# Output block products of an encoder layer: an earlier copy of a norm vector, a load in its place, and a new order of reads, gates and offsets

## The chip, the cores and the metric

The kernel runs on one core of a Trainium2 chip. The metric is the device time of one execution in microseconds (us). Five engines work side by side, each in the order of its own instructions: TensorE (PE; its weight loads are PEld), VectorE (DVE), ScalarE (ACT), GpSimd (POOL) and SyncE (SP), which only issues DMAs here. They wait for each other by semaphores.

## What is computed

The reference is one layer of a bidirectional encoder: an input projection, gated linear attention and latent attention side by side, then one output projection and a layer norm with a scaled residual. For this change the end matters:

```
mixed = concatenate([o_a, o_b], axis=-1) @ w_out        # 2048 x 1024 @ 1024 x 1024
x = layer_norm(DEEPNORM_ALPHA * x + mixed, ln_g, ln_b)
```

## The kernel before

Each float32 operand is split in a high part (a rounding copy, `K.hi`, mostly on ScalarE, line 396) and a low part (the rest, `K.lo`, mostly on GpSimd, line 402), and a product is three matmuls (`mm3`, lines 450 to 452): high x high, high x low, low x high.

The output projection works on 16 chunks of 128 rows. Chunks 0 to 7 are whole products: 2 halves of 512 columns, 8 blocks of 128 rows of the weights, 48 matmuls each. Chunks 8 to 15 go in four pairs (class `Pair`), pair p being chunks 9 + 2p (row 0) and 8 + 2p (row 1). A pair is a 2x2 block product made with seven half-size products instead of eight (12 matmuls each): A11 and A12 are the two attention outputs of row 0, A21 and A22 those of row 1, and

- S1 = A21 + A22, S3 = A11 - A21, S2 = S1 - A11, S4 = A12 - S2 are adds on VectorE (`add`, line 2016). S2 and S4 overwrite A11, S3 overwrites A21.
- The products in their order are P1 (operand A11), P5 (S1), P6 (S2), P3 (S4), P7 (S3), P2 (A12), P4 (A22); in the last pair P2 stands before P7 and P4 comes in two halves. They write the PSUM banks `pw`: P1 bank 0, P5 bank 1, P6 bank 2, P3 bank 3, P7 bank 0, P2 bank 1, P4 bank 3.
- VectorE adds them to the residual (`read`, lines 2051 and 2053: R1, R5, R5b, R2, R6, R3, R7, R4, R4b; U2 and U3, line 2044, combine two products in a bank). A bank can be written again only after its reads: P4 after R6 (the read of P3), P5 of the next pair after R7 (the read of P2).

P5 to P7 use weight combinations prepared earlier and fetched by `fetch_t` (names "1h" to "3l"); P4 uses "4h" and "4l", which overwrite half of `W`. "3l" lies in two tiles, `wt3l` and `wt3m`.

`Pair.load` brings a row's two attention outputs (`of`, from `oa_s` and `ob_s`) and its gates (`gr`, from `gm_s` and `r_s`) with four DMAs from SP. For pairs 0 and 2 `of` is a tile of a pool; for pairs 1 and 3 it is the place of the layer norm's vectors, `lng` for row 0 and `lnb` for row 1, free once `ln_psum` (line 2203, ScalarE) has copied them into PSUM. The `gr` of a row is the same place in every pair. `Pair.gate` (line 2004, GpSimd) multiplies the second attention output by the two gates.

The end of a chunk is a mean and variance, `finish_a` (lines 2312 to 2315, and `rsqrt`, lines 2321 to 2326 on ScalarE) or `squares`, `scale` and `centre` for row 0 of a pair, then `finish_b` (line 2332, VectorE): times the inverse deviation plus the offset `ln_b`, and a DMA to the output for each half. Row 0 of the last pair ends instead with `finish_first` (lines 2094 and 2095): ScalarE multiplies, GpSimd adds the offset from `lnbc`, a copy in SBUF (`copy_lnb`, line 2088).

The order is written out by hand. `PLACE_PAIR` gives each step of a pair a place in us relative to the pair's start T; all steps from chunk 6 on are sorted by place and held in that order on all five engines. The steps before (chunks 4 and 5, `split`, `finish`) are in program order on ScalarE, GpSimd and SP only. The places set the order alone: an engine waits for whatever its next instruction needs.

Of the kernel before, what the change touches and what calls it, by code (L numbers as in the profile page):

```python
# [9 lines left out]
F32 = mybir.dt.float32  # L10
F32R = mybir.dt.float32r
# [16 lines left out]
QB = 512  # L28
NQB = S // QB
NKT = S // P  # L30
# [65 lines left out]
    rcp=13.55,  # L96
# [11 lines left out]
    hi=(10.43, 11.83, 12.21, 14.39, 15.18, 22.96, 28.7, 34.03),  # L108
    lo=(15.35, 16.07, 20.38, 20.41, 24.45, 25.82, 33.5, 36.25),
# [24 lines left out]
PAIR0, PAIR_US = 8, 19.05  # L134
PLACE_PAIR = dict(
    load=(-31.0, -31.5),
    load1=(-23.6, -35.9),
    res=(-10.0, -8.0),
    gate=((-19.94, -18.58), (-24.72, -21.3)),
    add=dict(S1=-10.55, S3=-9.85, S2=-8.0, S4=-4.37),  # L140
    hi=dict(A11=-17.26, S1=-9.75, S2=-7.3, A12=-5.39, S3=-4.77, S4=-3.53, A22=-2.66),
    lo=dict(A11=-13.14, S1=-8.45, S2=-6.6, S3=-3.67, A22=1.77, A12=3.13, S4=4.49),
    product=dict(P1=0.0, P5=2.72, P6=5.44, P3=8.16, P7=10.88, P2=13.6, P4=16.32),
    last=dict(P1=0.0, P5=2.72, P6=5.44, P3=8.16, P2=10.88, P7=13.6, P4=16.32),
    gate1=((-14.6, -13.3), (-19.95, -18.6)),
    gate0=((-6.0, -4.7), (-24.72, -21.3)),
    first=dict(hA11=-15.2, hS3=-8.0, hA12=-2.6, lS3=-6.5, lS4=-2.2),
    read=dict(c1=2.78, R1=5.9, R5=6.5, R5b=7.1, U2=9.9, R2=10.5, R6=11.87, c7=14.91, U3=15.63, R3=16.26, bn22=16.89,
              R7=17.52, sq=18.25, R4=20.34, R4b=20.97, bn21=21.6, rs=21.9, fa=(22.9, 22.23), fb=(23.9, 26.7)),
    read_last=dict(c1=2.78, lnb=9.0, R1=3.3, R5=6.3, R5b=6.9, U2=8.9, R2=9.5, R3=10.1, R4b=10.7, R6=11.5, bn12=12.1,  # L150
                   R7=14.1, bn11=14.7, R3p=16.9, R4p=17.5, bn22=18.1, fa=(15.3, 20.2), fb=(17.0, 20.3)),
)

# [30 lines left out]
    vh=(0.732, 1.218),  # L184
# [26 lines left out]
    vl=(0.859, 1.227),  # L211
# [174 lines left out]
class K:  # L386
# [1215 lines left out]
    def attention(self):  # L1602
# [4 lines left out]
        with ExitStack() as ctx:  # L1607
# [220 lines left out]
            def put(place, fn, *a):  # L1828
                todo.append((place, len(todo), fn, a))
# [139 lines left out]
class Pair:  # L1969
# [12 lines left out]
    def load(self, r):  # L1982

        kern, nc, c = self.k, self.nc, self.c[r]
        b, cs = c // 4, slice((c % 4) * P, (c % 4 + 1) * P)
        if self.p % 2:
            of = self.op.ln_sb[r].rearrange("p a (b d) -> p a b d", b=4)
        else:
            of = kern.xfp.tile([P, 2, 4, P], F32, tag="xf", name=f"of{c}")
        self.of[r] = of  # L1990
        gr = self.rows[r]["gr"] = self.op.gr[c % 2]
        nc.sync.dma_start(of[:, 0], kern.oa_s[c])
        nc.sync.dma_start(gr[:, 0], kern.gm_s[b][:, :, cs])
        nc.sync.dma_start(gr[:, 1], kern.r_s[b][:, :, cs].to_broadcast([P, 4, P]))
        nc.sync.dma_start(of[:, 1], kern.ob_s[b][:, :, cs])
# [94 lines left out]
    def finish_first(self):  # L2090
        o, c = self.rows[0], self.c[0]
        for n in range(2):
            rr = o["rr"][:, n]
            self.nc.scalar.activation(rr, rr, AF.Copy, scale=o["rs"])
            self.nc.gpsimd.tensor_tensor(rr, rr, self.lnb[:, n], ALU.add)
            self.nc.sync.dma_start(self.k.out[c * P:(c + 1) * P, n * 512:(n + 1) * 512], rr)

    def put(self, put, T, last):
        at = lambda place, fn, *a: put(T + place, fn, *a)
        P_, op = PLACE_PAIR, self.op  # L2100
        first = {} if self.p else P_["first"]
        if self.p:
            for r in (1, 0):
                at(P_["load1" if self.p == 1 else "load"][r], self.load, r)
        for r in range(2):
            at(P_["res"][r], self.load_res, r)
            for n in range(2):
                at(P_[f"gate{self.p}" if self.p < 2 else "gate"][r][n], self.gate, r, n)
        for n in self.OPERANDS:
            if n[0] == "S":  # L2110
                at(P_["add"][n], self.add, n)
# [31 lines left out]
        at(e["lnb"], self.copy_lnb)  # L2143
# [14 lines left out]
class OutProj:  # L2158
# [47 lines left out]
    def fetch_t(self, n):  # L2206


        j, p = int(n[0]), "hl".index(n[1])
        src, kern = self.k.wt_s[j][p], self.k  # L2210
        if j == 4:
            for k in range(4):
                self.nc.sync.dma_start(self.W[k][p][:, 512:].bitcast(F32), src[:, k])
            return
        if n == "3l":
            t = [kern.wof.tile([P, D], F32R, tag="raw", name="wt3l", bufs=1).rearrange("p (a d) -> p a d", a=2),
                 kern.keep.tile([P, 2, QB], F32R, tag="acc", name="wt3m")]
            for i in range(2):
                self.nc.sync.dma_start(t[i].bitcast(F32), src[:, 2 * i:2 * i + 2])
        else:  # L2220
            slot = dict(zip(("1h", "1l", "2h", "2l", "3h"), ("ckvT_h", "ckvT_l", "krs", "vh", "vl")))[n]
            t = kern.rp.tile([P, NKT, P], F32R, tag=f"res_{slot}", name=f"wt{n}").rearrange("p (k a) d -> p k (a d)", k=4)
            self.nc.sync.dma_start(t.bitcast(F32), src)
            t = [t[:, 0:2], t[:, 2:4]]
        self.T[j, p] = t
# [67 lines left out]
    def residual(self, o, n):  # L2293
        nc, c = self.nc, o["c"]
        if n == 0:
            o["rr"] = self.bp.tile([P, 2, 512], F32, tag="ph", name=f"rr{c}", bufs=3)
            o["bn"] = self.sm.tile([P, 2, 6], F32, tag="bn", name=f"bn{c}")
        rr = o["rr"][:, n]
        nc.vector.scalar_tensor_tensor(rr, o["xr"][:, n], ALPHA, o["ps"][n], ALU.mult, ALU.add)
        nc.vector.bn_stats(o["bn"][:, n], rr)  # L2300

    def finish(self, o):
        self.finish_a(o)
# [98 lines left out]
```

## Time and profile before

| | us |
|---|---|
| median of 3 runs (1286.0 to 1287.68) | 1286.68 |
| the profiled execution | 1286.29 |
| its span, first to last instruction | 1284.5 |
| chunk 4 to the end, from | 1149.17 |
| pair 0 begins on TensorE | 1194.14 |
| pairs 1, 2, 3 begin | 1217.01, 1236.26, 1255.30 |
| last matmul begins | 1274.62 |

The times of instructions are counted from the start of the span, so the profiled execution is 1.8 us longer than what its trace shows. A line of a timeline gives the start, the duration, the engine, the line of the kernel, the operation, the tiles (out<-in), the shapes and the count, and in brackets the idle time before it and what ended it. A line of the DMA queue (SPq) is the issue; the transfer lands later.

### The profile page before, as it was taken

The page shows a single profiled execution, that of the slowest core. Times are in us where ns is not written, and L with a number is a line of the kernel's source. Part 1 is how long each engine was busy: PE and PEld are TensorE (multiplying, and loading weights), DVE is VectorE, ACT ScalarE, POOL GpSimd, SP SyncE. Part 2 cuts the span into 40 slices and gives each one's busy share as a digit, 9 for nine tenths or more (in the row PEclk, how much of TensorE's full clock was granted, in tenths as well). Part 3 has the DMA queues.
Part 4 walks back from the last instruction along what each step waited for, and adds up shares of the span by engine and source line. Part 5 has one row for each costly group of instructions (what it writes and reads, how often), then busy time and mean ns, then how long its engine had stood idle before and what let it go on. Part 6 is the DMA issues. An engine that isn't in the chain of part 4 may idle for free.

```text
span 1284.5 us, 20176 instructions
## 1 busy us (share of the span) xinstructions
PE 1257.6 (98%) x6928; PEld 1110.4 (86%) x6928; DVE 941.5 (73%) x1706; ACT 874.0 (68%) x1549; POOL 846.9 (66%) x546
## 2 busy tenths in 40 slices
PE   7999999999999999999999999999999999999997
PEld 7999999999889999999788888888888888888785
DVE  6865775656675455555798888888888888658788
ACT  7765657666675656665688888888888888614454
POOL 0244555363667666672188888889999999955762
PEclk9999999999999999999999999999999999999998
DMA  9332525353675565565501111122123211469952
GB/s 298 97 93 63 173 74 170 89 155 101 197 243 166 183 220 182 180 207 163 164 1 41 42 42 41 42 58 59 57 58 92 68 55 34 170 188 309 356 183 80
DMA packets 122518, 166.81 MB, mean 130 GB/s; under 512 B 18502, under 2 KB 71118, under 8 KB 121776
## 3 DMA queue, kind: packets, MB, share of 16 engines
q1 hardware_dynamic: 114256, 163.39, 40.2%
q0 software_dynamic: 768, 2.10, 0.5%
q8 instruction: 55, 0.90, 0.4%
q10 hardware_dynamic: 7392, 0.03, 0.3%
q14 instruction: 47, 0.39, 0.2%
HBM read 106.72 MB, written 58.75 MB: 129 GB/s over the span
## 4 chain that ended last, share of the span: by engine, by line
PE 56%; POOL 4%; issue 3%; DMA 3%; DVE 3%; ACT 3%; SPq 0%; DVEq 0%; POOLq 0%; ACTq 0%
PE pS L1636 4%; PE o L452 4%; PE o L450 4%; PE o L451 4%; PE pS L1637 4%; PE pS L1638 4%; PE pS L1639 4%; PE pS L1640 4%; PE pz L451 2%; PE pz L452 2%; PE pz L450 2%; PE ipm L452 1%; PE ipm L450 1%; PE ipm L451 1%; PE po L451 1%
## 5 line engine op out<-in xcount | busy, mean ns | idle before, releaser
L402 POOL TENSOR_TENSOR pl<-s,ph 128x1024 fp32r<-128x1024 f32 x128 | 306.1, 2416 | 56.6 <-ACT ph L396 56.6
L1658 DVE TENSOR_TENSOR rm<-pS,rm 128x512 f32<-128x512 f32 x210 | 144.8, 689 | 26.5 <-ACT s L1645 20.9
L1682 DVE TENSOR_TENSOR s<-s,mb 128x1024 f32<-128x1024 f32 x128 | 151.2, 1213 | 9.4 <-PE mb L1676 9.3
L1645 ACT ACTIVATE s<-pS 128x1024 f32<-128x1024 f32 x128 | 131.4, 1027 | 37.7 <-PE pS L1640 33.5
L396 ACT ACTIVATE ph<-s 128x1024 fp32r<-128x1024 f32 x128 | 134.9, 1057 | 13.5 <-PE o L452 12.9
L1686 ACT ACTIVATE s<-s 128x1024 f32<-128x1024 f32 x128 | 131.5, 1051 | 13.4 <-DVE s L1682 13.3
L450 PE MATMUL ipa<-wah,xah 128*128 128x384 f32 (+1 forms) x384 | 130.2, 339 | 6.1 <-ACT wah L396 6.0
L1099 POOL TENSOR_TENSOR Us<-Us,cw 128x512 f32<-128x512 f32 x16 | 18.6, 1163 | 174.2 <-DVE Us L1097 158.7
L451 PE MATMUL ipa<-wal,xah 128*128 128x384 f32 (+1 forms) x384 | 125.1, 326 | 0.2 <-DVE wal L402 0.2
L452 PE MATMUL ipa<-wah,xal 128*128 128x384 f32 (+1 forms) x384 | 125.2, 326 | 0.0
L1636 PE MATMUL pS<-qh,ckvT_h 128*128 128x512 f32 x256 | 102.6, 401 | 0.8 <-DVE rm L1658 0.4
L450 PE MATMUL o<-ph,vh 128*128 128x512 f32 x256 | 101.1, 395 | 0.0
L1637 PE MATMUL pS<-ql,ckvT_h 128*128 128x512 f32 x256 | 99.9, 390 | 0.0
L1638 PE MATMUL pS<-qh,ckvT_l 128*128 128x512 f32 x256 | 99.9, 390 | 0.0
L1639 PE MATMUL pS<-rh,krs 128*128 128x512 f32 x256 | 99.8, 390 | 0.0
L1640 PE MATMUL pS<-rl,krs 128*128 128x512 f32 x256 | 99.8, 390 | 0.0
L452 PE MATMUL o<-ph,vl 128*128 128x512 f32 x256 | 99.8, 390 | 0.0
L451 PE MATMUL o<-pl,vh 128*128 128x512 f32 x256 | 99.7, 389 | 0.0
L1709 DVE TENSOR_TENSOR ap<-ap,s 128x512 f32<-128x512 f32 x120 | 83.1, 692 | 3.5 <-ACT ap L1701 0.7
L450 PEld LDWEIGHTS ipa<-wah,xah 128*128 128x128 f32 x384 | 73.4, 191 | 6.9 <-ACT wah L396 6.3
L450 PE MATMUL pz<-xch,wzh 128*128 128x256 f32 x256 | 74.8, 292 | 0.0
L451 PEld LDWEIGHTS ipa<-wal,xah 128*128 128x128 f32 x384 | 73.4, 191 | 1.2 <-DVE wal L402 0.6
(446 smaller groups left out, 3897.7 us busy)
## 6 DMA issues: line engine op xcount, KB each, us to landing
xcf<-xT_dram SPq DMA_DIRECT2D x16, 512.0 KB, 4.6
xr<-x_dram SPq DMA_DIRECT2D x16, 512.0 KB, 6.3
xaf<-xT_dram SPq DMA_DIRECT2D x14, 512.0 KB, 3.7
wb<-wO_dram SPq DMA_DIRECT2D x16, 256.0 KB, 3.5
oib<-oi_s SPq DMA_DIRECT2D x16, 256.0 KB, 4.3
qdb<-qd_s SPq DMA_DIRECT2D x16, 256.0 KB, 5.1
SU<-su_s SPq DMA_DIRECT2D x16, 256.0 KB, 4.5
ub<-u_s SPq DMA_DIRECT2D x16, 256.0 KB, 4.7
```

The source lines that it names most:

```text
L396: return nc.scalar.activation(dst, src, AF.Copy).ins
L402: return e.tensor_tensor(dst, src, hi.bitcast(F32), ALU.subtract).ins
L450: mm(out, ah, bh, start=start, stop=False)
L451: mm(out, ah, bl, start=False, stop=False)
L452: mm(out, al, bh, start=False, stop=stop)
L1636: mm(ps[:, e], kh, qh, start=True, stop=False)
L1637: mm(ps[:, e], kh, ql, start=False, stop=False)
L1638: mm(ps[:, e], kl, qh, start=False, stop=False)
L1639: mm(ps[:, e], kr, rh, start=False, stop=False)
L1640: mm(ps[:, e], kr, rl, start=False, stop=True)
L1658: V.tensor_tensor(d["rm"], src[:, e], d["rm"], ALU.max)
L1682: V.tensor_tensor(s, s, d["mb"][:, None, :].to_broadcast([P, 2, QB]), ALU.subtract)
```

## The change

- `ln_psum(0)` moves from the sorted steps (place 2.0) into chunk 4's block, behind chunk 6's operands; chunk 5's bank is taken just before it, so that the PSUM places stay as they were. Right behind it SP loads the two halves of `of` of pair 1's row 0 into `lng`. Its gates follow at place -23.7.
- The gates of pair 1's row 0 move on GpSimd from -14.6 and -13.3 to -7.9 and -6.6, that is behind A11l and S1l and just ahead of S2l.
- Pair 2's row 0 is loaded at -25.5 instead of -31.0, behind pair 1's two residual loads.
- R6 (the read of P3, the fourth product) moves from 11.87 to 11.3, and S2 from -8.0 to -7.6 of the next pair (19.05 later), so that R6 now stands before S2.
- `fetch_t`: the first tile of "3l" is fetched behind the norm vectors during the attention, the second ("3m") behind pair 0's loads; "4h" and "4l" at 17.15 instead of 21.9.
- The offsets of pair 2 (chunks 13 and 12) go by `finish_off`, the former `finish_first`, on ScalarE and GpSimd; `copy_lnb` moves from 9.0 to -1.5 of the last pair.
- `rcp` of the last attention block is held behind the last statistics of chunk 4.

```diff
 PLACE_PAIR = dict(
     load=(-31.0, -31.5),
-    load1=(-23.6, -35.9),
+    load2=(-25.5, -31.5),
+    load1=(-23.7, -35.9),
...
-    add=dict(S1=-10.55, S3=-9.85, S2=-8.0, S4=-4.37),
-    hi=dict(A11=-17.26, S1=-9.75, S2=-7.3, A12=-5.39, S3=-4.77, S4=-3.53, A22=-2.66),
-    lo=dict(A11=-13.14, S1=-8.45, S2=-6.6, S3=-3.67, A22=1.77, A12=3.13, S4=4.49),
+    add=dict(S1=-10.55, S3=-9.85, S2=-7.6, S4=-4.37),
+    hi=dict(A11=-17.26, S1=-9.75, S2=-7.0, A12=-5.39, S3=-4.77, S4=-3.53, A22=-2.66),
+    lo=dict(A11=-13.14, S1=-8.45, S2=-6.5, S3=-3.67, A22=1.77, A12=3.13, S4=4.49),
...
-    gate1=((-14.6, -13.3), (-19.95, -18.6)),
+    gate1=((-7.9, -6.6), (-19.95, -18.6)),
...
-    read=dict(c1=2.78, R1=5.9, R5=6.5, R5b=7.1, U2=9.9, R2=10.5, R6=11.87, c7=14.91, ...
+    read=dict(c1=2.78, R1=5.9, R5=6.5, R5b=7.1, U2=9.9, R2=10.5, R6=11.3, c7=14.91, ... late=(24.2, 24.8)),
+    lnb=-1.5,
...
+                    put(max(lo, end + 26) + 0.03, op.fetch_t, "3l")
...
+                    if c == 4:
+                        rest[5]["ps"] = op.banks(rest[5])
+                        op.ln_psum(0)
+                        pairs[1].load(0, "of")
                     pairs[0].load(1 if c == 4 else 0)
                     if c > 4:
                         tsum(nb - 1)
-                        rcp(nb - 1)
+                        with self.after(rest[4]["last"]):
+                            rcp(nb - 1)
+                        op.fetch_t("3m")
...
-            put(2.0, op.ln_psum, 0)
             put(3.5, op.ln_psum, 1)
-            put(1.0, op.fetch_t, "3l")
-            put(21.9, op.fetch_t, "4h")
-            put(21.91, op.fetch_t, "4l")
+            put(17.15, op.fetch_t, "4h")
+            put(17.16, op.fetch_t, "4l")
...
-                at(P_["load1" if self.p == 1 else "load"][r], self.load, r)
+                at(P_[f"load{self.p}" if self.p < 3 else "load"][r], self.load, r, *(("gr",),) * (self.p == 1 and r == 0))
...
             for r in range(2):
-                at(e["fb"][r], op.finish_b, self.rows[r])
+                if op.last_pair.p == self.p + 1:
+                    at(e["late"][r], op.last_pair.finish_off, self.rows[r])
+                else:
+                    at(e["fb"][r], op.finish_b, self.rows[r])
```

More of the change, by code (lines that the diff above doesn't have):

```diff
@@ L136 @@
     load=(-31.0, -31.5),
-    load1=(-23.6, -35.9),
+    load2=(-25.5, -31.5),
+    load1=(-23.7, -35.9),
     res=(-10.0, -8.0),
     gate=((-19.94, -18.58), (-24.72, -21.3)),
-    add=dict(S1=-10.55, S3=-9.85, S2=-8.0, S4=-4.37),
-    hi=dict(A11=-17.26, S1=-9.75, S2=-7.3, A12=-5.39, S3=-4.77, S4=-3.53, A22=-2.66),
-    lo=dict(A11=-13.14, S1=-8.45, S2=-6.6, S3=-3.67, A22=1.77, A12=3.13, S4=4.49),
+    add=dict(S1=-10.55, S3=-9.85, S2=-7.6, S4=-4.37),
+    hi=dict(A11=-17.26, S1=-9.75, S2=-7.0, A12=-5.39, S3=-4.77, S4=-3.53, A22=-2.66),
+    lo=dict(A11=-13.14, S1=-8.45, S2=-6.5, S3=-3.67, A22=1.77, A12=3.13, S4=4.49),
     product=dict(P1=0.0, P5=2.72, P6=5.44, P3=8.16, P7=10.88, P2=13.6, P4=16.32),
     last=dict(P1=0.0, P5=2.72, P6=5.44, P3=8.16, P2=10.88, P7=13.6, P4=16.32),
-    gate1=((-14.6, -13.3), (-19.95, -18.6)),
+    gate1=((-7.9, -6.6), (-19.95, -18.6)),
     gate0=((-6.0, -4.7), (-24.72, -21.3)),
+    second={},
     first=dict(hA11=-15.2, hS3=-8.0, hA12=-2.6, lS3=-6.5, lS4=-2.2),
-    read=dict(c1=2.78, R1=5.9, R5=6.5, R5b=7.1, U2=9.9, R2=10.5, R6=11.87, c7=14.91, U3=15.63, R3=16.26, bn22=16.89,
-              R7=17.52, sq=18.25, R4=20.34, R4b=20.97, bn21=21.6, rs=21.9, fa=(22.9, 22.23), fb=(23.9, 26.7)),
-    read_last=dict(c1=2.78, lnb=9.0, R1=3.3, R5=6.3, R5b=6.9, U2=8.9, R2=9.5, R3=10.1, R4b=10.7, R6=11.5, bn12=12.1,
+    read=dict(c1=2.78, R1=5.9, R5=6.5, R5b=7.1, U2=9.9, R2=10.5, R6=11.3, c7=14.91, U3=15.63, R3=16.26, bn22=16.89,
+              R7=17.52, sq=18.25, R4=20.34, R4b=20.97, bn21=21.6, rs=21.9, fa=(22.9, 22.23), fb=(23.9, 26.7), late=(24.2, 24.8)),
+    lnb=-1.5,
+    read_last=dict(c1=2.78, R1=3.3, R5=6.3, R5b=6.9, U2=8.9, R2=9.5, R3=10.1, R4b=10.7, R6=11.5, bn12=12.1,
                    R7=14.1, bn11=14.7, R3p=16.9, R4p=17.5, bn22=18.1, fa=(15.3, 20.2), fb=(17.0, 20.3)),
@@ L1956, in attention @@
                 put(place, f, nb - 1)
-            put(2.0, op.ln_psum, 0)
             put(3.5, op.ln_psum, 1)
-            put(1.0, op.fetch_t, "3l")
-            put(21.9, op.fetch_t, "4h")
-            put(21.91, op.fetch_t, "4l")
+            put(17.15, op.fetch_t, "4h")
+            put(17.16, op.fetch_t, "4l")
+            op.last_pair = pairs[-1]
             for q in pairs:
@@ L1980, in __init__, with load @@
         self.of, self.h, self.l, self.begun = [None, None], {}, {}, set()
-    def load(self, r):
+    def load(self, r, what=("of", "gr")):
         kern, nc, c = self.k, self.nc, self.c[r]
         b, cs = c // 4, slice((c % 4) * P, (c % 4 + 1) * P)
[L1986 to L1995, printed above, removed]
+        if "of" in what:
+            if self.p % 2:
+                of = self.op.ln_sb[r].rearrange("p a (b d) -> p a b d", b=4)
+            else:
+                of = kern.xfp.tile([P, 2, 4, P], F32, tag="xf", name=f"of{c}")
+            self.of[r] = of
+            nc.sync.dma_start(of[:, 0], kern.oa_s[c])
+        if "gr" in what:
+            gr = self.rows[r]["gr"] = self.op.gr[c % 2]
+            nc.sync.dma_start(gr[:, 0], kern.gm_s[b][:, :, cs])
+            nc.sync.dma_start(gr[:, 1], kern.r_s[b][:, :, cs].to_broadcast([P, 4, P]))
+        if "of" in what:
+            nc.sync.dma_start(of[:, 1], kern.ob_s[b][:, :, cs])
     def load_res(self, r):
@@ L2088, in copy_lnb, with finish_off @@
         self.nc.scalar.activation(self.lnb, self.op.ln[1], AF.Copy)
-    def finish_first(self):
-        o, c = self.rows[0], self.c[0]
+    def finish_off(self, o):
+        c = o["c"]
         for n in range(2):
@@ L2100, in put @@
         P_, op = PLACE_PAIR, self.op
-        first = {} if self.p else P_["first"]
+        first = P_[("first", "second")[self.p]] if self.p < 2 else {}
         if self.p:
             for r in (1, 0):
-                at(P_["load1" if self.p == 1 else "load"][r], self.load, r)
+                at(P_[f"load{self.p}" if self.p < 3 else "load"][r], self.load, r, *(("gr",),) * (self.p == 1 and r == 0))
         for r in range(2):
@@ L2110, in put @@
             if n[0] == "S":
-                at(P_["add"][n], self.add, n)
+                at(first.get(f"a{n}", P_["add"][n]), self.add, n)
             at(first.get(f"h{n}", P_["hi"][n]), self.hi, n)
@@ L2140, in put @@
             for r in range(2):
-                at(e["fb"][r], op.finish_b, self.rows[r])
+                if op.last_pair.p == self.p + 1:
+                    at(e["late"][r], op.last_pair.finish_off, self.rows[r])
+                else:
+                    at(e["fb"][r], op.finish_b, self.rows[r])
             return
-        at(e["lnb"], self.copy_lnb)
+        at(P_["lnb"], self.copy_lnb)
         at(e["bn12"], self.stats, 0, 1, 1)
@@ L2152, in put @@
         at(e["fa"][0], op.finish_a, self.rows[0])
-        at(e["fb"][0], self.finish_first)
+        at(e["fb"][0], self.finish_off, self.rows[0])
         at(e["fa"][1], op.finish_a, self.rows[1])
@@ L2206, in fetch_t @@
     def fetch_t(self, n):
-        j, p = int(n[0]), "hl".index(n[1])
-        src, kern = self.k.wt_s[j][p], self.k
+        kern, sync = self.k, self.nc.sync
+        j = int(n[0])
         if j == 4:
+            p = "hl".index(n[1])
             for k in range(4):
-                self.nc.sync.dma_start(self.W[k][p][:, 512:].bitcast(F32), src[:, k])
+                sync.dma_start(self.W[k][p][:, 512:].bitcast(F32), kern.wt_s[j][p][:, k])
             return
[L2215 to L2225, printed above, removed]
+        if n in ("3l", "3m"):
+            i = "lm".index(n[1])
+            if i:
+                t = kern.keep.tile([P, 2, QB], F32R, tag="acc", name="wt3m")
+            else:
+                t = kern.wof.tile([P, D], F32R, tag="raw", name="wt3l", bufs=1).rearrange("p (a d) -> p a d", a=2)
+            sync.dma_start(t.bitcast(F32), kern.wt_s[j][1][:, 2 * i:2 * i + 2])
+            self.T[j, 1] = self.T.get((j, 1), []) + [t]
+            return
+        p = "hl".index(n[1])
+        slot = dict(zip(("1h", "1l", "2h", "2l", "3h"), ("ckvT_h", "ckvT_l", "krs", "vh", "vl")))[n]
+        t = kern.rp.tile([P, NKT, P], F32R, tag=f"res_{slot}", name=f"wt{n}").rearrange("p (k a) d -> p k (a d)", k=4)
+        sync.dma_start(t.bitcast(F32), kern.wt_s[j][p])
+        self.T[j, p] = [t[:, 0:2], t[:, 2:4]]
     def wt(self, j, k):
@@ L2299, in residual @@
         nc.vector.scalar_tensor_tensor(rr, o["xr"][:, n], ALPHA, o["ps"][n], ALU.mult, ALU.add)
-        nc.vector.bn_stats(o["bn"][:, n], rr)
+        o["last"] = nc.vector.bn_stats(o["bn"][:, n], rr).ins
     def finish(self, o):
```

## Prediction

> **What bounds the kernel now.** I read the page first, then the stretches at the end and the waits of TensorE, and last the timelines of the engines from 1120 us on. P1 to P7 are the seven products of a pair of chunks; "pair 0" is chunks 9 and 8, "pair 3" is 15 and 14; S4h and S4l are the high and the low part of operand S4. Times are us from the start of the span.
>
> ```profile
> span 1284.5 us, 20176 instructions
> PE 1257.6 (98%) x6928; PEld 1110.4 (86%) x6928; DVE 941.5 (73%) x1706; ACT 874.0 (68%) x1549; POOL 846.9 (66%) x546
> ```
> TensorE (PE) is busy 98% of the span, so a gain can come only from where it stands still, where its clock is low, and what runs after its last matmul. For the stage that the change touches:
>
> ```profile
> PE pw L450 <- DVE xr L2053: 1.9, 1, 1.9
> ...
> 1209.47:1212.88 3.41, 1.47 (x7) 0.91 (x6) 2.34 (x2) 0.94 (x2) 2.12 (x3) 1.00 1.06 350
> 1212.88:1216.29 3.41, 3.41 (x9) 2.64 (x8) 2.25 (x4) 2.37 (x5) 1.90 (x2) 0.50 1.09 308
> ...
> 1194.14 0.39 PE L450 MATMUL pw<-woh,A11h 128*128 128x512 f32 x1
> 1210.24 0.39 PE L452 MATMUL pw<-woh,A12l 128*128 128x512 f32 x1
> 1212.57 0.55 PE L450 MATMUL pw<-woh,A22h 128*128 128x512 f32 x1 [1.94 <-DVE xr L2053]
> 1217.01 0.40 PE L450 MATMUL pw<-woh,A11h 128*128 128x512 f32 x1
> ```
> There is one long wait: P4 of pair 0 waits 1.94 us for VectorE's read of its bank. In the second window (the columns are PE, weight load, DVE, ACT, POOL, granted clock, DMA share, GB/s) stands a second price: the next 3.41 us run at clock 0.50. From 1194.14 to 1210.24 are 71 steps of 0.2268 us; the 84 matmuls of a pair take 19.04 us, and pair 1 would begin at 1213.18, not 1217.01. **Stall and slow clock together cost 3.83 us.**
>
> Why that read is late, on VectorE (DVE) and GpSimd (POOL):
>
> ```profile
> 1210.17 1.74 DVE L2016 TENSOR_TENSOR lng<-s,lng 128x512 f32<-128x512 f32 x1 [2.47 <-POOL A11l L402]
> 1211.83 0.68 DVE L2053 TENSOR_TENSOR xr<-pw,xr 128x512 f32<-128x512 f32 x1
> 1213.97 0.69 DVE L2016 TENSOR_TENSOR lng<-lng 128x512 f32<-128x512 f32 x1 [1.46 <-POOL S2l L402]
> ...
> 1202.86 1.29 POOL L402 TENSOR_TENSOR A12l<-of,A12h 128x512 fp32r<-128x512 f32 x1
> 1205.80 3.08 POOL L2004 TENSOR_TENSOR lng<-lng,gr 128x512 f32<-128x512 f32 x2 [1.65 <-DMA lng<-ob_s]
> 1208.84 1.29 POOL L402 TENSOR_TENSOR A11l<-lng,A11h 128x512 fp32r<-128x512 f32 x1
> 1215.45 1.29 POOL L2004 TENSOR_TENSOR of<-of,gr 128x512 f32<-128x512 f32 x1 [1.51 <-DMA of<-ob_s]
> 1217.95 3.93 POOL L2004 TENSOR_TENSOR of<-of,gr 128x512 f32<-128x512 f32 x3
> 1224.35 1.30 POOL L402 TENSOR_TENSOR S4l<-lng,S4h 128x512 fp32r<-128x512 f32 x1
> ```
> The read (R6, 1211.83) stands behind the add S2 of pair 1; S2 overwrites A11 in place and waits for A11l; A11l stands behind two gates that waited for a load into `lng`.
>
> The end has another bound:
>
> ```profile
> 1263.77 1.40 DVE L2332 SCALAR_TENSOR_TENSOR xr<-xr,ln_r,ln 128x512 f32<-128x512 f32 x2
> 1266.29 1.40 DVE L2332 SCALAR_TENSOR_TENSOR xr<-xr,ln_r,ln 128x512 f32<-128x512 f32 x2
> 1277.10 0.41 DVE L2053 TENSOR_TENSOR xr<-pw,xr 128x256 f32<-128x256 f32 x1
> ...
> 1265.00:1278.35 13.35, 9.90 (x56) 8.49 (x54) 13.04 (x27) 4.04 (x10) 2.49 (x2) 0.98 0.24 90
> ...
> 1274.62 0.28 PE L452 MATMUL pw<-woh,A22l 128*128 128x256 f32 x1
> ```
> VectorE is busy 13.04 of 13.35 us there. TensorE is done at 1274.90, yet VectorE comes to its last result only at 1277.10: it is 2.2 us behind. The 7.4 us from there to the end the change leaves alone.
>
> **The change part by part.**
>
> *R6 before S2, gates later, half of a load sooner.* A11l no longer stands behind the gates: it can start when A12l of pair 0 ends, at 1204.15, and ends at about 1205.4. S1, which waits for nothing else that is late, comes then (the two engines exclude each other on such adds, as S2 took 1.74 us beside a GpSimd operation and the like one at 1213.97 took 0.69); S3, U2 and R2 follow at 0.7 us each, and R6 runs from about 1208.2 to 1208.9, ahead of P4, due at 1210.46. If all comes 1 us later (below) it still fits. **Worth at P4: 3.83 us**, if nothing is late next.
>
> *The Trainium skill*, page "TensorE: Matmul & The Clock Gate", section "HAM oscillation — how this bites in real kernels", puts the loss of clock at idle gaps over about 3.4 us. By that rule this edit would be worth 1.94 us; the trace has clock 0.50 after a gap of 1.94 us, and the measurement decides.
>
> *What is late next: S4l of pair 1.*
>
> ```profile
> 1225.70 0.50 PE L452 MATMUL pw<-woh,S4l 128*128 128x512 f32 x1
> ...
> 1213.74 1.23 SPq L2000 DMA_DIRECT2D xr<-x_dram  x2
> ...
> xr<-x_dram SPq DMA_DIRECT2D x1, 512.0 KB, 6.1
> ...
> 1208.00:1212.00 4.00, 2.63 (x12) 1.85 (x10) 1.83 (x2) 0.06 (x1) 3.36 (x3) 1.00 1.05 377
> ```
> P3 of pair 1 took S4l at 1225.70, 0.05 us after GpSimd had made it (1224.35 + 1.30): the present stall hides a second one. With pair 1 at 1213.18 that matmul, the 39th of its pair, is due at 1221.8. GpSimd makes eight operations from pair 2's first gate (1215.45) to S4l, 10.2 us; from the gates of pair 2's row 0 (the second of three at 1217.95, so 1219.25) to the end of S4l are 6.4 us. So two bounds:
> - GpSimd alone: S1 until 1206.1, S1h 0.7, S1l until 1208.1, two gates with S2 between them until 1211.2, S2l until 1212.5, then 10.2 us and some contention: 1223.0. A wait of 1.2 us.
> - The load of pair 2's row 0. The DMA engines are full (share 1.05, 377 GB/s). The first `xr` load, issued at 1213.74, landed 6.1 us later, at 1219.84; its 512 KB take 1.4 us at that rate, so the row-0 load ahead of it landed at about 1218.45. The change takes 512 KB (half of wt3l) and 512 KB (`lng`) out of the queue ahead of it and puts the two `xr` loads, 1024 KB, in: net nothing. I take 1218.45, with 1217 and 1220.5 as ends: a bit over 1 us where the queue could be filled better, 2 us where SP is held up (pair 0's loads, below, and the `gr` place that row 0 shares with the later gates). S4l is ready 6.45 us after it, at 1224.9.
>
> I take the second, the longer: P3 goes on at 1224.95, 0.75 us sooner than before, **after a new wait of 3.15 us**. Whether the clock drops again:
>
> ```profile
> 223.02:226.43 3.41, 2.20 (x12) 1.68 (x11) 3.35 (x3) 2.50 (x7) 1.66 (x1) 1.00 0.78 215
> ```
> a window with 2.20 us of work kept the clock, that with 1.47 lost it. However the windows cut a wait of 3.15 us, one of them keeps at most 1.84 us of work, in most cuts under 1.47. I count one window at 0.50, 1.7 us. Of the 3.83 us, 3.15 go back as a wait and 1.7 as clock.
>
> *VectorE's round.*
>
> ```profile
> 1230.53 0.68 DVE L2016 TENSOR_TENSOR of<-s,of 128x512 f32<-128x512 f32 x1
> 1231.13 0.69 DVE L2053 TENSOR_TENSOR xr<-pw,xr 128x512 f32<-128x512 f32 x1
> 1233.29 1.76 DVE L2016 TENSOR_TENSOR of<-of 128x512 f32<-128x512 f32 x1 [1.48 <-POOL S2l L402]
> 1237.03 0.68 DVE L2053 TENSOR_TENSOR xr<-pw,xr 128x512 f32<-128x512 f32 x1
> 1257.41 0.67 DVE L2053 TENSOR_TENSOR xr<-pw,xr 128x512 f32<-128x512 f32 x1
> 1258.13 0.50 PE L450 MATMUL pw<-wt1h,S1h 128*128 128x512 f32 x1
> ```
> From R7 to R7 (1237.03, 1257.41) VectorE needs 20.38 us, TensorE 19.04; at 1258.13 P5 of pair 3 starts just as R7 frees its bank. With R6 first (now 1231.13) S2 starts 0.6 us later, and S4 waits for S2h and S2l behind it: two rounds grow by 0.6 us each. Against that S4 of pair 1 (1213.97) comes at about 1212.5, up to 1.5 us sooner, or no sooner if a gate is ahead of it as at 1233.29. R7 of pair 2 ends between 1257.8 and 1259.3. From TensorE's side P5 is due 142 steps after the matmul at 1225.70, 32.2 us (it took 32.4): 1224.95 + 32.2 + 1.7 = 1258.85. The two run side by side and do not add.
>
> *Offsets of pair 2 on ScalarE and GpSimd.* VectorE loses the four instructions at 1263.77 and 1266.29, 2.8 us. ScalarE (4.04 of 13.35 us busy) gets four copies of 128x512, GpSimd (2.49) four adds of at most 1.3 us, and only output DMAs wait for them. VectorE catches up, and TensorE's end sets the last read. Without that cover VectorE would be as late as now.
>
> *The rest.*
>
> ```profile
> 1170.88 0.63 ACT L396 ACTIVATE oh<-of 128x512 fp32r<-128x512 f32 x1 [4.62 <-POOL of L2250]
> 1180.45 1.01 ACT L2203 ACTIVATE ln<-lng 128x1024 f32<-128x1024 f32 x1
> ...
> 1179.01 1.66 POOL L402 TENSOR_TENSOR ol<-of,oh 128x512 fp32r<-128x512 f32 x1 [0.74 <-ACT oh L396]
> ...
> 1121.45 0.36 SPq L2194 DMA_DIRECT2D lnb<-ln_b_dram  x1
> 1130.10 0.33 SPq L2263 DMA_DIRECT2D xr<-x_dram  x1
> ```
> The copy of `lng` moves on ScalarE from 1180.45 to behind 1170.88 and makes what follows 1.0 us later. Chunk 7's last part is then ready at 1181.7, not 1180.7; TensorE wants it 36 matmuls before 1194.14, at 1186.0. SP gets two more issues there and sends pair 0's loads 1 us later; 12 us remain. Half of wt3l at about 1122 finds SP idle until 1130. The sooner copy for the offsets is one instruction of 1.0 us. I set all this at nothing; bounds 0 and 1 us.
>
> **The sum.** TensorE's end: 1224.95 + (1274.90 - 1225.70) + 1.7, less the 0.2 lost before P5 of pair 3 = 1275.65. The last read starts at 1275.7, not 1277.10: **1.4 us sooner**. The profiled execution took 1286.29 with its span of 1284.5; that makes 1284.9, and 1285.3 from the median of the runs, 1286.68. I forecast 1285.1, a gain of 0.1%: the stall comes back at the fourth product of the next pair, and what stays is VectorE's lead at the end.
>
> **Rivals.**
> - *No second loss of clock* (the wait short, or cut by the windows). From TensorE's side P5 of pair 3 is then due at 1257.15, from R7 at 1257.85 at the earliest; TensorE ends 16.7 us after it (1274.90 - 1258.13, less 0.1), at 1274.5, and the whole is 2.5 us or somewhat more sooner: 1283.8. For it: the early end of the load. Against: clock 0.50 after 1.94 us. The skill's limit of 3.4 us for idle gaps (page "TensorE: Matmul & The Clock Gate") would bring this case even with the wait of 3.15 us. Chance 0.22.
> - *Slower: pair 2's row 0 lands late*, at P3 of pair 1, because two `xr` loads stand ahead of it on SP in a full queue and its `gr` place is freed by later gates. Each us of landing is a us at P3. From 1219.9 on the gain is gone; at 1221.5 it costs 1.6 us (1288.2), from 1222.5 over 0.2%. For: share 1.05. Against: the bytes ahead are equal. Chance 0.17.
> - *The stall at P4 stays*, R6 being late behind S1 and S3. Under 1 us it is swallowed by that at P3; all of it leaves the end, 2.2 us of VectorE's delay less 1.2 for the longer rounds: 1285.5. Chance 0.06.
>
> **Chances.** Forecast 0.55 (its own range 1284.2 to 1286.6). About 0.2% (2.6 us) is what a measurement of this kernel can tell from no change. Faster by more: most of the first rival, 0.2. Slower by more: the far part of the second, or clock lost in two windows, 0.13. Within: 0.67. The range takes in most of both: 1283.0 to 1288.2.
>
> **What would show it.** Right: no wait of P4 of pair 0, and clock 1.00 after it; a wait on S4l at P3 of pair 1, and GpSimd's gates on `of` waiting for a DMA just before; a window at 0.50 behind it; R6 ahead of S2; VectorE at its last read within 0.2 us of TensorE's end. Wrong: S4l ready before 1223, or no slow window; then the gain is nearer 3 us. A wait in chunk 6 or 7 would mean that the moved copy or loads cost what I set at nothing.

## The result and the profile after

The changed kernel takes 1293.43 us (median of 4 runs, 1292.25 to 1294.3), the kernel before 1286.77 beside it: 1.0051 times the time, 95% interval 1.0033 to 1.0068. It is **slower by 6.7 us**, where I forecast 0.1% faster and a range up to 1288.2.

The page's first lines and TensorE's waits from 1140 us on:

```profile
span 1292.5 us, 20183 instructions
...
PE 1259.5 (97%) x6928; PEld 1112.4 (86%) x6928; DVE 938.3 (73%) x1702; ACT 876.4 (68%) x1553; POOL 850.1 (66%) x550
...
PE pmb L453 <- ACT oh L399: 6.7, 1, 6.7
PE pw L455 <- POOL S4l L405: 2.3, 1, 2.3
PE pw L453 <- DVE xr L2065: 0.4, 1, 0.4
PE pmb L455 <- POOL ol L405: 0.3, 1, 0.3
```

The wait of P4 of pair 0 is gone, and the two that I named, P3 of pair 1 for S4l and P5 of pair 3 for R7, are there. But the longest wait stands where I had expected none: `pmb` is the bank of chunk 6, ahead of the pairs. TensorE's timeline:

```profile
1151.00 0.39 PE L453 MATMUL pmb<-woh,oh 128*128 128x512 f32 x1
...
1169.17 0.80 PE L453 MATMUL pmb<-woh,oh 128*128 128x512 f32 x1 [6.69 <-ACT oh L399]
1170.68 0.79 PE L455 MATMUL pmb<-woh,ol 128*128 128x512 f32 x1 [0.28 <-POOL ol L405]
...
1173.63 0.40 PE L453 MATMUL po<-woh,oh 128*128 128x512 f32 x1
...
1205.07 0.39 PE L453 MATMUL pw<-woh,A11h 128*128 128x512 f32 x1
1221.39 0.39 PE L453 MATMUL pw<-woh,A22h 128*128 128x512 f32 x1
1224.11 0.39 PE L453 MATMUL pw<-woh,A11h 128*128 128x512 f32 x1
1235.14 0.50 PE L455 MATMUL pw<-woh,S4l 128*128 128x512 f32 x1 [2.26 <-POOL S4l L405]
1268.05 0.50 PE L453 MATMUL pw<-wt1h,S1h 128*128 128x512 f32 x1 [0.43 <-DVE xr L2065]
```

At 1151.00 chunk 4 begins. Then come matmuls of chunk 6 (1169.17), and only behind them chunk 5's product (`po`, 1173.63). Nine matmuls of chunk 6 (three blocks of its first half) stand ahead of a whole product that could have run, and wait for chunk 6's operands. Before, chunk 5 began at 1160.42, straight behind chunk 4. The wait also costs clock, as the windows of 3.41 us show (PE, weight load, DVE, ACT, POOL, granted clock, DMA share, GB/s):

```profile
1163.12:1166.53 3.41, 0.00 (x0) 0.00 (x0) 3.41 (x7) 0.00 (x0) 0.00 (x0) 1.00 0.75 210
1166.53:1169.95 3.42, 0.78 (x2) 0.50 (x2) 3.42 (x7) 2.01 (x7) 0.76 (x1) 0.50 1.03 337
1169.95:1173.36 3.41, 3.13 (x8) 2.15 (x7) 2.72 (x6) 0.00 (x0) 3.33 (x3) 0.50 1.01 420
1173.36:1176.78 3.42, 3.42 (x16) 2.82 (x15) 1.41 (x2) 2.92 (x9) 1.59 (x2) 1.00 1.00 379
```

Stage by stage, from the starts of the first matmuls (one profiled execution of each kernel; the columns from e1 on are experiments told below):

| us | before | after | e1 order | e2 copy alone | e5 bank | e6 + S4l | e9 + R6 back | e10 + S4 |
|---|---|---|---|---|---|---|---|---|
| chunk 4 to pair 0 | 44.97 | 54.07 | 46.12 | 54.16 | 45.88 | 45.23 | 46.42 | 45.76 |
| pair 0 | 22.87 | 19.04 | 19.04 | 19.04 | 20.05 | 19.08 | 19.33 | 19.76 |
| pair 1 | 19.25 | 21.59 | 25.92 | 19.60 | 26.67 | 19.96 | 20.94 | 20.75 |
| pair 2 | 19.04 | 19.04 | 19.04 | 19.34 | 19.04 | 21.21 | 20.38 | 20.18 |
| pair 3 to the last matmul | 19.32 | 19.80 | 19.08 | 19.43 | 19.08 | 20.64 | 19.46 | 19.08 |
| last matmul to the end | 9.88 | 7.96 | 7.96 | 9.92 | 7.99 | 7.92 | 7.94 | 7.99 |

After less before: 9.10 - 3.83 + 2.34 + 0 + 0.48 - 1.92 = 6.17 us, near the 6.7 of the medians. (The two profiled executions are 8.01 us apart; the other 1.83 had come up before chunk 4 began.) The part that I had set at nothing took 9.1 us. The other rows are 2.9 us shorter together, but that is not yet the worth of the parts that I had worked on: e2, which has none of them, gains as much there.

### The profile page after: what moved, and what is told of

Read it like the earlier page. It is cut to its first block, busy times and chain, and to the rows that moved or that the text cites. A ratio compares the mean times of both kernels' runs of the same rounds, so it can differ in the third digit from the quotient of the medians.

```text
span 1292.5 us, 20183 instructions
## 1 busy us (share of the span) xinstructions
PE 1259.5 (97%) x6928; PEld 1112.4 (86%) x6928; DVE 938.3 (73%) x1702; ACT 876.4 (68%) x1553; POOL 850.1 (66%) x550
## 4 chain that ended last, share of the span: by engine, by line
PE 62%; POOL 3%; issue 2%; DVE 2%; ACT 2%; DMA 1%; SPq 0%; DVEq 0%; POOLq 0%; ACTq 0%
PE o L455 4%; PE o L453 4%; PE pS L1639 4%; PE o L454 4%; PE pS L1640 4%; PE pS L1641 4%; PE pS L1643 4%; PE pS L1642 4%; PE pz L454 2%; PE pz L455 2%; PE pz L453 2%; PE ipm L455 1%; PE ipm L453 1%; PE ipm L454 1%; PE pw L455 1%
## 5 line engine op out<-in xcount | busy, mean ns | idle before, releaser
L1689 ACT ACTIVATE s<-s 128x1024 f32<-128x1024 f32 x128 | 131.5, 1051 | 13.4 <-DVE s L1685 13.3
```

## The experiments

The first theory, A: nine matmuls placed ahead are the loss. Its rival, B: the moved copy and loads delay chunk 6's operands, whatever TensorE's order. TensorE's order around chunks 4 and 5 is the builder's choice, since the kernel holds only ScalarE, GpSimd and SP in order there. Four kernels were run beside 29 runs of the kernel before (1287.72, 1285.08 to 1289.19).

**e1, TensorE's old order.**

```diff
-                with fixed():
+                with (fixed() if c == 4 else self.in_order(late, LATE_ORDER + ENGINES[:1])):
```

> The changed kernel with one thing put back: TensorE's instructions of chunk 5's block are held in program order, so that all of chunk 5's product stands before chunk 6's again; everything else is as in the changed kernel. Theory A (the 6.8 us are lost because nine matmuls of chunk 6 were placed ahead of chunk 5 and wait there for chunk 6's operands): in the changed kernel's trace pair 0 begins 54.07 us after chunk 4 (1205.07 - 1151.00), before 44.97 (1194.14 - 1149.17); 9.1 us of that go, and the rest of the change stays, which is 2.9 us from pair 0 to the end (87.43 against 90.36). About 1283.9 us, 1283 to 1285.6; no wait of TensorE over 0.5 us before pair 0; P4 of pair 0 waits for nothing; P3 of pair 1 still waits 2 to 3 us for S4l. Theory B (the earlier copy and load delay chunk 6's operands or fill the queue, whatever TensorE's order): chunk 5 or 6 still waits, and the time stays above 1288.

Measured: 1288.65 us, 1.0009 (1.0000 to 1.0018). The nine matmuls are back behind chunk 5 and 4.8 us are won, yet it is no faster than before. Theory A had 1283 to 1285.6 and missed. B's signs came, a wait and over 1288 us, but not its cause: chunk 5 waits, and not for chunk 6's operands. Waits of TensorE, its first matmul of chunk 5, and VectorE:

```profile
PE pw L455 <- POOL S4l L405: 4.0, 1, 4.0
PE po L453 <- DVE rr L2318: 1.0, 1, 1.0
...
1164.77 0.47 PE L453 MATMUL po<-woh,oh 128*128 128x512 f32 x1 [1.04 <-DVE rr L2318]
...
1163.34 1.29 DVE L2318 SCALAR_TENSOR_TENSOR rr<-xr,po 128x512 f32<-128x512 f32 x2 [0.16 <-PE px L455]
```

The two residuals that read a bank `po` end at 1164.63, and the matmul starts at 1164.77. They are chunk 3's. In the trace of before the same two stand beside chunk 5's matmuls:

```profile
1160.20 1.28 DVE L2299 SCALAR_TENSOR_TENSOR rr<-xr,po 128x512 f32<-128x512 f32 x2
...
1160.42 0.48 PE L450 MATMUL po<-woh,oh 128*128 128x512 f32 x1
```

There TensorE writes chunk 5's bank from 1160.42 on while VectorE still reads chunk 3's until 1161.48, so these are two banks. In e1 TensorE waits for that read, as it must if both are one bank. So the theory became: **the early copy of `lng` takes the free one of two PSUM places, the one that chunk 1 had, and chunk 5's product gets the place of chunk 3, which VectorE reads late.** The line of the change that takes chunk 5's bank just ahead of the copy does not keep the places as they were. That the copy has the place of chunk 1 is inferred from the waits; e5 tests it.

**e2, the copy alone; e3, the copy alone with the old order.** The kernel before, with chunk 5's bank and `op.ln_psum(0)` moved into chunk 4's block and nothing else; e3 holds TensorE's order as e1 does.

> The kernel before with one step of the change alone: the copy of the norm vector into PSUM, with chunk 5's bank taken ahead of it, in chunk 4's block; no load, gate, read or offset is moved. Theory A: this step alone puts the nine matmuls of chunk 6 ahead of chunk 5, with a wait of 5 to 7 us there and two windows at half clock: chunk 4 to pair 0 takes 54 us and not 45, so 1295.9 if P4 of pair 0 stalls as before (3.8 us), 1292 if the loads now come early enough for it. Theory B (the order comes from the load of the attention output or from the wait put on rcp): TensorE's order as before, and 1286 to 1288.

> The same, the kernel before with the early copy alone, but TensorE's instructions of chunk 5's block held in program order. Theory A (the order costs, not the copy): chunk 4 to pair 0 takes 45 us again and the time is that of the kernel before, 1286 to 1288. Theory B (the copy itself delays ScalarE and what waits for it): within 1 us of the kernel with the copy alone.

Measured: e2 1293.06 us, 1.0042 (1.0030 to 1.0055), with 6.3 us of waiting for chunk 6's `oh` and 54.16 us from chunk 4 to pair 0; e3 1288.26, 1.0004 (0.9996 to 1.0013), with 1.9 us of chunk 5 waiting for `rr`. From chunk 4 to pair 0 e3 takes 47.01 us, where theory A had 45: of the 9.19 us the order is 7.15, and that wait is nearly all of the rest. Lines of e2, where `lng` is copied to `ln`:

```profile
PE pmb L450 <- ACT oh L396: 6.3, 1, 6.3
...
1165.93 0.80 PE L450 MATMUL pmb<-woh,oh 128*128 128x512 f32 x1 [6.34 <-ACT oh L396]
...
1170.99 1.01 ACT L2205 ACTIVATE ln<-lng 128x1024 f32<-128x1024 f32 x1
```

One instruction of 1.0 us, moved, is the whole loss between chunk 4 and pair 0. Its own duration has no part in the wait: it runs at 1170.99, when the wait is over.

The column of e2 shows something else. Its stages add up to 6.16 us over before, those of the changed kernel to 6.17, and the two times, 1293.06 and 1293.43, agree within their runs. Pair 0 takes 19.04 us in e2 too, with R6, gates and loads in their old places: TensorE comes about 8 us later, and R6 is done when P4 starts. So behind the late start all other parts of the change together were worth nothing, 2.0 us lost at pair 1 and 2.0 won at the end.

**e4, S4l first** (`second=dict(lS4=-2.0)`, with e1's order). In the changed kernel S4l stands on GpSimd behind the gates of pair 2's row 0, A22l and A12l, none of which P3 of pair 1 needs.

> The changed kernel with TensorE's old order in chunk 5's block and, besides, the low part of S4 of pair 1 earlier on GpSimd: ahead of the gates of pair 2's row 0 and of A22l and A12l. S4h is ready at 1222.7 in the changed kernel's trace, S4l was made only at 1233.8, behind gates that waited for a load until 1228.7. Theory A (GpSimd's order holds S4l): P3 of pair 1 waits for nothing, S4l being ready some 4 us ahead of it. What that is worth has two readings. A1, TensorE carries it to the end: 2.3 us under the kernel with the old order alone, about 1281.6. A2, VectorE's round is next (P5 of pair 3 waited 0.43 us for R7 already): P5 of pair 3 then waits 2 to 2.7 us for R7 and the time is within 0.5 us of the kernel with the old order alone, about 1283.9.

Measured: 1286.61 us, 0.9994 (0.9986 to 1.0002). No wait for S4l is left; P5 of pairs 2 and 3 wait up to 1.3 us for R7. A2 fits in kind, the wait moves on to VectorE, but not in size (it had 1283.9): chunk 5 waits 2.4 us for `rr` here and 49.08 us pass from chunk 4 to pair 0.

The next four ran beside the kernel before at 1287.53 (34 runs).

**e5, the bank mended.** The copy is written into the tile that chunk 3's product had:

```diff
-                        rest[5]["ps"] = op.banks(rest[5])
-                        op.ln_psum(0)
+                        op.ln_psum(0, rest[3]["pt"])
```

> The changed kernel with the early copy written into the bank that chunk 3's product had, so that chunk 5's product keeps the bank that chunk 1 had; nothing else is changed, and no order is held that was free. Theory A (the early copy takes the bank that is free, so chunk 5's product gets chunk 3's, which VectorE reads late; both the wait of 1.0 to 2.4 us for VectorE with the old order and the nine matmuls placed ahead come from that): TensorE's order is the old one by itself, chunk 5 begins behind chunk 4 without a wait, chunk 4 to pair 0 takes 45.0 us and not 54.1 or 46.1 to 49.1. P4 of pair 0 waits for nothing, P3 of pair 1 waits 3 to 4.5 us for S4l with one or two windows at half clock, and the end is 1.9 us shorter: 1 to 2 us under the run with the old order alone, 1286.0 to 1287.5 where the kernel before has 1287.7. Theory B (VectorE is late at chunk 4 for another reason, the copy or the loads): the wait before chunk 5 stays, and so does the time of that run, 1288.6.

Measured: 1288.59 us, 1.0011 (1.0003 to 1.0020). Theory A's mechanism holds, its time (1286.0 to 1287.5) does not. With no order held, TensorE's is the old one by itself, and chunk 5 starts beside chunk 3's residuals:

```profile
1159.24 0.48 PE L453 MATMUL po<-woh,oh 128*128 128x512 f32 x1
...
1159.97 1.28 DVE L2317 SCALAR_TENSOR_TENSOR rr<-xr,po 128x512 f32<-128x512 f32 x2
```

From chunk 4 to pair 0 are 45.88 us; of the 0.9 over before, chunk 7 waits 0.5 for `yc`, as it also does in e8 without the early copy. The time is that of e1: what chunk 5 no longer loses goes at pairs 0 and 1, most of it at P3 of pair 1; GpSimd and TensorE:

```profile
1215.65 1.29 POOL L2015 TENSOR_TENSOR of<-of,gr 128x512 f32<-128x512 f32 x1 [2.20 <-DMA of<-ob_s]
1216.89 1.31 POOL L405 TENSOR_TENSOR S3l<-lnb,S3h 128x512 fp32r<-128x512 f32 x1
1218.15 1.32 POOL L2015 TENSOR_TENSOR of<-of,gr 128x512 f32<-128x512 f32 x1
1221.39 2.64 POOL L2015 TENSOR_TENSOR of<-of,gr 128x512 f32<-128x512 f32 x2 [1.93 <-DMA of<-ob_s]
1224.00 1.26 POOL L405 TENSOR_TENSOR A22l<-lnb,A22h 128x512 fp32r<-128x512 f32 x1
1225.22 1.27 POOL L405 TENSOR_TENSOR A12l<-lng,A12h 128x512 fp32r<-128x512 f32 x1
1226.45 1.26 POOL L405 TENSOR_TENSOR S4l<-lng,S4h 128x512 fp32r<-128x512 f32 x1
...
1227.77 0.80 PE L455 MATMUL pw<-woh,S4l 128*128 128x512 f32 x1 [4.69 <-POOL S4l L405]
...
1223.70:1227.10 3.40, 0.00 (x0) 0.00 (x0) 3.40 (x6) 0.68 (x3) 3.40 (x4) 0.81 0.73 212
1227.10:1230.50 3.40, 2.73 (x7) 2.15 (x8) 3.37 (x4) 0.63 (x1) 3.40 (x3) 0.50 0.92 256
```

The gates of pair 2's row 0 start at 1221.39, when the load lands; S4l comes 6.3 us later, as I had worked out (6.45), but from a landing that is 3 us later than mine. The wait is 4.69 us, the clock falls to half, and pair 1 takes 26.67 us: 4.69 of waiting and 2.9 of clock over 19.04, where I had 1.7 of clock. SP issues the last load of that row at 1214.57, against 1213.16 before, and the loads of `of` take 5.7 to 6.8 us from issue to landing, against 5.2 to 5.9. So part of the lateness is SP's and part the queue's.

**e6, the bank mended and S4l first.**

> The same with the low part of S4 of pair 1 ahead of the gates of pair 2's row 0 on GpSimd. Theory A: neither chunk 5 nor P3 of pair 1 waits; what is left are the waits of P5 of pairs 2 and 3 for R7, since VectorE's round takes 21.2 us (R7 at 1241.23 and 1262.40 in the run with S4l first) and TensorE's 19.04. Against that run, where chunk 4 to pair 0 took 49.1 us, 2.4 to 4 us less: 1282.5 to 1284.2, or 1284.9 if VectorE's round takes back part. Theory B (waiting at chunk 5 had only hidden VectorE's round): no less than 1286.

Measured: 1286.09 us, 0.9991 (0.9982 to 1.0000). Neither chunk 5 nor P3 waits any more, yet it is over what theory A gave, and theory B's bound holds. R7 of pairs 1 and 2:

```profile
1237.28 0.67 DVE L2064 TENSOR_TENSOR xr<-pw,xr 128x512 f32<-128x512 f32 x1
1258.46 0.67 DVE L2064 TENSOR_TENSOR xr<-pw,xr 128x512 f32<-128x512 f32 x1
...
PE pw L453 <- DVE xr L2064: 2.8, 3, 1.3
```

VectorE's round of 21.18 us is now what a pair costs: pairs 1 and 2 take 19.96 and 21.21 where TensorE needs 19.04. In e1 and e5 the long wait at P3 had hidden it.

**e7, pair 2's offsets on VectorE again** (`if False:` in place of the test for the last pair, on e5).

> The changed kernel with the bank mended, but pair 2's offsets on VectorE as before (no copies on ScalarE, no adds on GpSimd for them). Theory A (the offsets are worth VectorE's lag at the end): from the last matmul's start to the end of the span about 9.9 us and not 7.9 to 8.1, so 1.9 us over the run with the bank mended. Rival (TensorE's end is late enough here that VectorE catches up anyway): less than 0.5 us over it.

Measured: 1290.07 us, 1.0016 (1.0008 to 1.0025), 1.5 over e5 by the medians, with intervals that overlap. In the trace the last read starts 1.34 us after TensorE's end (1281.97 against 1280.35 + 0.28), in e5 0.18, and the stretch from the last matmul to the end is 9.05 us against 7.99. That is 1.1 us and not the 1.9 of theory A: here VectorE is less far behind TensorE at the end than it was before.

**e8, R6 alone** (places of R6 and S2 of the change, on the kernel before).

> The kernel before with one step of the change alone: R6 ahead of S2 on VectorE (and S2's parts at their new places); gates, loads, copy and offsets as before. Theory A (P4 of pair 0 waits only because R6 stands behind S2): its wait of 1.9 us and the half clock behind it go, 3.8 us; S4l then makes P3 of pair 1 wait 3 us or more, with or without a window at half clock, and the time is 0 to 2 us under that of before, 1285.7 to 1287.7. Rival (R6 is late behind S1 and S3 too, since the gates still stand ahead of A11l): P4 of pair 0 still waits over 1 us and the time is that of before.

Measured: 1290.13 us, 1.0020 (1.0011 to 1.0029): slower by 2.6, which neither theory had. P4 of pair 0 waits no more, P3 of pair 1 waits 1.8 us for S4l, but P5 waits for R7 (1.5 us in two), and pair 1 takes 21.75 us. R7 of pair 2 comes 21.17 us after that of pair 1 (1242.10, 1263.27), against 20.38 before: R6 ahead of S2 is enough to lengthen VectorE's round.

The last runs ask what R6 ahead of S2 does to VectorE's round. e9 to e11 stand beside 1287.06 (21 runs), e12 beside 1286.77 (15 runs).

**e9, e6 with R6 behind S2 again** (R6 at 11.87, S2 at -8.0).

> The run with the bank mended and S4l first, and R6 behind S2 again, as in the kernel before. Theory A (R6 ahead of S2 lengthens VectorE's round: before, R6 filled part of the time in which VectorE waits for S2l, 1.5 us of waiting were left and R7 came every 20.38 us; with R6 first 2.1 us are left and R7 comes every 21.17): R7 comes every 20.4 us again, the waits of P5 of pairs 2 and 3 shrink, and the time is 1.2 to 2 us under that run's 1286.1, about 1284.5; P4 of pair 0 still waits for nothing, because A11l no longer stands behind the gates. Rival (R6 ahead of S2 is what keeps P4 of pair 0 from waiting): P4 waits over 1 us, the clock drops, and the time is 1287 or more.

Measured: **1284.70 us, 0.9984 (0.9976 to 0.9993)**, as theory A had it. It is faster than the kernel before, by an interval that excludes no change, and its slowest run (1287.24) lies below the changed kernel's fastest (1292.25). Against e6 the gain is not clear by the times alone, since the two intervals overlap. P4 of pair 0 waits for nothing, so with the gates behind A11l R6 needs no earlier place. R7 of pair 2 comes 20.41 us after that of pair 1, as before the change:

```profile
1237.34 0.67 DVE L2064 TENSOR_TENSOR xr<-pw,xr 128x512 f32<-128x512 f32 x1
1257.75 0.67 DVE L2064 TENSOR_TENSOR xr<-pw,xr 128x512 f32<-128x512 f32 x1
...
PE pw L453 <- ACT S2h L399: 1.6, 2, 1.2
```

The last line is P4 of pairs 1 and 2. S2h is no operand of P4; R6 stands behind S2 on VectorE there and ends about when S2h does.

**e10, S4 behind U3 and R3** (S4 at -2.75, its high part at -2.7, on e9).

> The same with the add S4 on VectorE behind U3 and R3 of the pair before (and its high part behind it), so that VectorE works while S2l is made. Theory A (VectorE's round is the bound of the pairs now): R7 comes every 19.0 to 19.5 us, no P5 waits over 0.5 us, pairs 1 to 3 begin 19.04 to 19.5 us apart, and the time is 1281.5 to 1283.5. Rival (S4 is then late for P3): P3 waits for S4h or S4l in pairs 2 and 3, and nothing is gained over the run before.

Measured: 1284.94 us, 0.9983 (0.9974 to 0.9992), the same as e9. VectorE's wait for S2l is gone, and a new one has its place:

```profile
DVE pw L2055 <- ACT pc L2052: 6.9, 3, 3.6
```

U3 needs `pc`, ScalarE's copy of P7, which stands on ScalarE behind S2h, A12h and S3h, and S2h waits for S2 on VectorE. R7 of pair 2 comes 19.35 us after that of pair 1, as theory A had it, but that of pair 1 20.27 after pair 0's. The rival's wait at P3 came to no more than 0.2 us; the gain did not come either.

**e12, the same with R6 first.**

> The run with the bank mended, S4l first and S4 behind U3 and R3, but with R6 ahead of S2 as the change has it. In the two runs before, with R6 behind S2, P4 of pairs 1 and 2 waited 1.2 and 0.8 us in the longest case for R6 (what is named there is S2h, which ends just before). Theory A (R6 ahead of S2 is good where VectorE need not wait for S2l, and bad where it does): P4 waits for nothing, R7 comes no later than in the run with S4 behind R3 (19.4 to 20.3 us), pairs begin under 20.2 us apart, and the time is 1283.5 to 1284.5. Rival (R6 first lengthens VectorE's round wherever S4 stands): 1285.5 to 1286.5.

Measured: 1286.07 us, 0.9993 (0.9984 to 1.0002): the rival's time, though the interval overlaps that of e10. Counted from the start of pair 1, S2 of pair 2 begins at 18.77 us (1232.69 - 1213.92) and at 16.50 in e10 (1231.30 - 1214.80), and `pc` is as much later: R6 ahead of S2 makes S2, and with it `pc`, later with S4 behind R3 too.

**e11, pair 2's row-0 load back in its old place** (on e5).

> The run with the bank mended (gates of pair 2's row 0 still ahead of S4l), and pair 2's row-0 load back ahead of pair 1's two residual loads on SP. Theory A (S4l waits for that load, which is late because 1024 KB of residuals go ahead of it; it landed at 1221.4, 1.9 us after GpSimd was free, and S4l waited for it): the gates start 1.5 to 2.5 us sooner, P3 of pair 1 waits 2.5 to 3.2 us and not 4.7, and the time is 1 to 2.5 us under that run's 1288.6 if the residuals do not become late. Rival (gr's place is free only after pair 1's gates, so SP stands still there and all that follows, the residuals too, is late): R1 of pair 1 waits for its residual, and the time is 1288.6 or more.

Measured: 1295.87 us, 1.0070 (1.0058 to 1.0083). It answers another question than mine: with pair 1's row-0 gates moved behind that load in the program, they take the gate values of pair 2, and wait for them (VectorE waits 9.8 us for S2l). That is another computation than the reference's. So it shows that the load had to move with the gates, and nothing on what the residual loads ahead of it cost. That was not tried in another way.

## Why the prediction was wrong

**The step that failed** is "The rest", where I wrote of the moved copy, the loads and what goes with them: "I set all this at nothing; bounds 0 and 1 us". I had priced the copy as 1.0 us of ScalarE's time and followed what it delays on ScalarE. I had not asked which PSUM place it fills and who wanted that place, nor who fixes TensorE's order in a block where only three engines are held. Moved, the copy cost 9.1 us from chunk 4 to pair 0. e2 shows it with nothing else changed, e3 that the order is most of it (7.15 of 9.19 us), e5 that the place is behind both. That the builder put the nine matmuls ahead because it reckoned with the wait for chunk 3's bank fits all runs, but is argued: its reckoning is in no trace. My last sentence named the sign ("a wait in chunk 6 or 7 would mean ..."), yet no rival had it with a price.

Point by point:

- *P4 of pair 0, 3.83 us*: right in kind, but the changed kernel does not show it. Its pair 0 takes 19.04 us (1205.07 to 1224.11), and so does that of e2, by TensorE's lateness alone. The runs in which TensorE comes about as early as before do show it: P4 waits for nothing in e5, e6 and e9, and pair 0 takes 19.08 to 20.05 us. The cause was only half named: gates behind A11l, with half of that load sooner, do it without R6 (e9), R6 does it without the gates (e8).
- *S4l at P3 of pair 1, 3.15 us and 1.7 of clock*: right in kind, mis-sized. In the changed kernel it is 2.26 us at full clock, since TensorE came 9 us later. With the order or the bank put right it is 4.0 us (e1), 4.69 (e5) and 5.4 (e7), and pair 1 takes 6.9 to 8.8 us over 19.04, where I had 4.85. The landing was mis-sized: 1221.39 and not 1218.45, past my later end of 1220.5. That is the second rival, to which I gave 0.17; it put 1288.2 beside a landing at 1221.5, and e5 came to 1288.59. Even without the bank the change would have been no faster. Why SP issues the load later, and why it then takes longer, stays open.
- *VectorE's round, 0.6 us*: right in kind. R7 in the changed kernel:

```profile
1246.14 0.67 DVE L2065 TENSOR_TENSOR xr<-pw,xr 128x512 f32<-128x512 f32 x1
1267.33 0.67 DVE L2065 TENSOR_TENSOR xr<-pw,xr 128x512 f32<-128x512 f32 x1
...
1284.54 0.28 PE L455 MATMUL pw<-woh,A22l 128*128 128x256 f32 x1
...
1285.01 0.41 DVE L2065 TENSOR_TENSOR xr<-pw,xr 128x256 f32<-128x256 f32 x1
```

  It takes 21.19 us, 0.8 over before, and P5 of pair 3 waits 0.43. I counted it as a side condition; it is the next bound. Where P4 of pair 0 and P3 of pair 1 had lost their long waits (e4, e6, e9, e10, e12), pairs 1 and 2 took 40.2 to 42.8 us together, and TensorE needs 38.1.
- *The offsets, 2.2 us*: right for the changed kernel. The last read starts 0.19 us behind TensorE's end (1284.82), and the end is 1.9 us nearer. On e5 they are worth 1.1 us in that stretch (e7).
- *The rivals*: none ended at 1293. In the changed kernel no clock is lost at P3, as the first had it, but that decided nothing.

## What to carry to other kernels

An instruction that is moved sooner also takes its buffer sooner: before it is priced by its duration, ask which place it fills, who had it next, and which engines' order is free to be rearranged around it. And an edit that shortens one wait should be followed to the engine whose round is next: here the wait at P4 hid that at P3, and that at P3 hid VectorE's round, so that in the traces of before and e9 pair 0 and the end became 5.5 us shorter, the other stages 4.6 us longer. By the medians 2.4 us stayed.

## What the runs showed of the hardware

The granted clock does not follow from a wait's length alone. A wait of 1.94 us cost a window at half clock before; 2.26 us at P3 in the changed kernel cost none, nor did 1.93 us at chunk 5 in e3 (11.00 us from there to chunk 6, against 10.97 before); 2.42 us at chunk 5 in e4 did (12.58 us). What fits these four is the work left in a window of 3.41 us, counted from the edges at which the clock changes in the same trace. The windows ahead of half clock held 1.47 us of TensorE's work (before) and 0.99 (e4). Those that kept the clock held 2.23 or more (e3) and about 1.5 (the changed kernel); these two are estimates, since their windows are counted over 55 and 65 us from the nearest edge. If there is a limit, it lies near 1.5 us in these traces, but no run was made to test it. By the Trainium skill, page "TensorE: Matmul & The Clock Gate", section "HAM oscillation — how this bites in real kernels", gaps over about 3.4 us lose the clock; the waits of 4.69 and 6.69 us agree, and so do 1.93 and 2.26 us, which lost none; those of 1.94 and 2.42 us do not.

Runs of the kernel before scatter by 4 us (1285.08 to 1289.19), and chunk 4 begins between 1147.99 (e5) and 1152.68 (e8), ahead of nearly all that was changed. So a stage's time was taken from its own start, and a kernel's from medians. Where the scatter comes from was not followed.
